# FFN layer one: an inner seven-product scheme over both token pairs for two of its seven products

## The chip, the cores and the metric

The kernel runs on one core of a Trainium2 chip. The metric is the device time of one execution in microseconds (us); less is better.

## The reference

One decoder block over 2048 tokens of width 1024, all in float32. What matters here is the feed-forward part at its end:

```
h  = x + concat[RMSNorm(PoolMix(u)), RMSNorm(StickBreakAttn(q, k, v))] @ W_out
h  = h + relu(RMSNorm(h) @ W_up) ** 2 @ W_down        # W_up 1024 x 4096, W_down 4096 x 1024
y  = RMSNorm_final(h)
```

Layer one is `relu(RMSNorm(h) @ W_up) ** 2`, layer two the product with `W_down` and the final norm.

## The kernel before

**Tokens and tiles.** The tokens are four tiles of T = 512, j = 0 to 3. Activations lie with features on the 128 partitions, so a piece is 128 x 512, 256 KB in float32. Matrices are multiplied to float32 accuracy by splitting each operand into a high and a low part (`split`, lines 140 to 144: ScalarE copies the high part, line 143; VectorE subtracts it, line 144). Each 128x128 by 128x512 block product is then three matmuls: high by high, high by low, low by high.

**Seven products.** Both feed-forward layers use a seven-product scheme of the Strassen-Winograd kind over a 2 x 2 split of tokens and of features. `PAIRS = ((0, 1), (3, 2))`: pair q = 0 is the tiles 0 and 1, pair q = 1 the tiles 3 and 2. Of the normed rows of a pair seven left operands are made (A11, A12, A22 and the sums S1 to S4), each of 512 features, that is four pieces; of the four quarters of `W_up` for a column m (0 to 15: 128 columns of its left half and the same 128 of its right half) come seven right operands. The products P1 to P7 go to three PSUM accumulators: Y takes P1, P6, P7, P4; Z takes P5, P3; X takes P2. The four results of a column are squared after relu and combined at once to the left operands of layer two, written to `sd` in DRAM.

**Layer one before, `up`.** The loop runs over `cols`, pair by pair, 16 columns each, and within a column over the seven products (`slots`, with the next column's P1 put ahead of P4). Each slot is 12 matmuls (four pieces by three) in line 1016. `load` (line 876) fetches 1 MB of `W_up` for each pair and column; `add_weights` (lines 880 to 883) makes the weight sums; `make_weights` splits them (tiles `hw`), `UA` = 4 slots ahead. `make_left` (its load is line 899) loads and splits the left operands of a pair (`sr`, `sa`). `post` reads the accumulators: copies of Y in ScalarE (line 955), sums with X and Z (lines 961, 969, 985), relu and square (lines 949, 950), outputs (line 946). During pair 0, `sums_second` norms and sums the rows of pair 1 (lines 911 to 917; tiles `hn`) and keeps them in `su`. Their norm needs the root of tiles 2 and 3: `root_last` (matmuls pm, then a chain of small operations in GpSimd, lines 208 to 218 and 815, 816) and `spread` (matmuls pr, line 225), in the slots g = 1, 6 and 10.

**Order.** Work is written in program order, but the order on each engine, and on SP's queue that issues the DMAs, comes from a scheduler which goes by its own estimate of when operands and buffers are ready; program order only sets who goes first among the ready. Pools are stacked in SBUF; a tile of a pool that is opened later waits for those tiles of closed pools whose place it takes. `begin_ffn` opens the pools of `up` while the out projection's last tile still runs (lines 172 to 174 are its matmuls, `add_acc` its sums), and `up` stops at its `yield` until `ffn` goes on with it. `down` (line 1251, its loads `wr`, `ar`) follows.

Of the kernel before, what the change touches and what calls it, by code (L numbers as in the profile page):

```python
# [8 lines left out]
F32 = mybir.dt.float32  # L9
# [16 lines left out]
G = 4  # L26
# [10 lines left out]
SR = 4  # L37
LB = 4
UA = 4
LA = 5  # L40
# [6 lines left out]
def hymba_block(ctx: ExitStack, tc: tile.TileContext, xT, gains, w_in, pool_w, w_out, w_up, w_down, out):  # L47
# [87 lines left out]
    su = [[[dram.tile([P, 2, T], F32, name=f"su{q}_{i}_{c}") for c in range(2)] for i in range(7)] for q in range(2)]  # L135
# [719 lines left out]
    def up(pools, more):  # L855

        saps, hlp, rba, rtp, srp = pools
        NM = NF // 2
        cols = [(q, m) for q in range(2) for m in range(NM)]

        what = {"P1": (A11, (0, 0), "Y", True, False), "P2": (A12, (0, 1), "X", True, True),
                "P6": (S2, (1, 1), "Y", False, False), "P5": (S1, (1, 0), "Z", True, False),
                "P7": (S3, (1, 2), "Y", False, False), "P4": (A22, (1, 3), "Y", False, True),
                "P3": (S4, (0, 2), "Z", False, True)}
        order = list(what)

        slots = [cols[0] + ("P1",)]
        for n, c in enumerate(cols):
            slots += [c + (s,) for s in ("P2", "P6", "P5", "P7")]
            slots += [c2 + ("P1",) for c2 in cols[n + 1:n + 2]]  # L870
            slots += [c + (s,) for s in ("P4", "P3")]
        raw, sums, ops, left_ops, ps, keep = {}, {}, {}, {}, {}, {}

        def load(q, m):
            raw[q, m] = (rbb if m % 2 else rba).tile([P, 4, G, P], F32, tag="rb", name="rb")
            nc.sync.dma_start(raw[q, m], w_up[m])

        def add_weights(q, m):
            b, t = raw[q, m], rtp.tile([P, 4, G, P], F32, tag="rt", name="rt")
            nc.vector.tensor_tensor(t[:, 0], b[:, 3], b[:, 0], ALU.subtract)  # L880
            nc.vector.tensor_tensor(t[:, 1], b[:, 2], t[:, 0], ALU.subtract)
            nc.vector.tensor_tensor(t[:, 2], b[:, 2], b[:, 3], ALU.subtract)
            nc.vector.tensor_tensor(t[:, 3], b[:, 1], t[:, 1], ALU.subtract)
            sums[q, m] = t

        def make_weights(g):
            q, m, s = slots[g]
            which, i = what[s][1]
            if s == "P2":
                add_weights(q, m)  # L890
            hl = hlp.tile([P, 2, G, P], F32R, tag="hw", name="hw", align_bytes=256)
            split((hl[:, 0], hl[:, 1]), (sums if which else raw)[q, m][:, i])
            ops[g] = hl

        def make_left(q, s):
            i, parts = what[s][0], []
            for c in range(2):
                r = srp.tile([P, 2, T], F32, tag="sr", name="sr")
                nc.sync.dma_start(r, su[q][i][c])
                t = saps[order.index(s)].tile([P, 2, 2, T], F32R, tag="sa", name="sa", align_bytes=256)  # L900
                split((t[:, 0], t[:, 1]), r)
                parts.append(t)
            left_ops[q, s] = parts

        SUMS, second = ("P2", "P5", "P4"), {}

        def sums_second(n, part):

            c, k = n // 2, n % 2
            new = lambda name: avp.tile([P, T], F32, tag="av", name=name)  # L910
            keep = lambda i, t: nc.sync.dma_start(su[1][i][c][:, k], t)
            add = lambda to, x, y, op: nc.vector.tensor_tensor(to, x, y, op)

            def normed_of(h, i):
                t, j = new("hn"), PAIRS[1][h]
# [513 lines left out]
```

## Time and profile before

| | |
|---|---|
| runs | 1950.17, 1945.07, 1943.7 us; median 1945.07 |
| span of the profiled execution | 1941.4 us |
| granted TensorE clock, mean | 0.998 |
| TensorE busy | 1922.7 us, 9139 matmuls |
| VectorE busy | 1267.6 us |
| ScalarE busy | 956.9 us |
| moved by DMA | 426.79 MB, mean 220 GB/s |
| matmuls of layer one (line 1016) | 2688, from 694.5 to 1309 us |

The span runs from the first to the last instruction of one profiled execution. The time of the profiled execution itself isn't listed apart from its span, so the prediction goes from the span to the median by their difference. Busy times count a matmul from its start to its modelled end, and since matmuls overlap, the distance between starts says more than the durations. The same holds for the other engines' back-to-back operations.

### The profile page before, as it was taken

The numbers are of one execution on the slowest core, as the hardware profiler recorded it, in microseconds if no ns is written. First come the engines' busy times: TensorE is split into PE (matmuls) and PEld (weight loads), VectorE is DVE, ScalarE is ACT, GpSimd is POOL, SyncE is SP. The second block draws the span as 40 slices with busy tenths as digits, with TensorE's granted clock in tenths as the row PEclk, the third lists the DMA queues.
The fourth block names the chain that finished last, engine by engine and source line by source line (L and its number), as shares of the span: only waits on it lengthen the run. The fifth ranks groups of instructions, "written<-read, shape, count | busy, mean of one in ns | idle before, by whom it ended". The sixth has DMA issues, their size and how long they took to land.

```text
span 1941.4 us, 25998 instructions
## 1 busy us (share of the span) xinstructions
PE 1922.7 (99%) x9139; PEld 1605.2 (83%) x9139; DVE 1267.6 (65%) x1882; ACT 956.9 (49%) x1544; POOL 192.0 (10%) x399
## 2 busy tenths in 40 slices
PE   9999999999999999999999999999999999999997
PEld 7888888888888888888888888878888888888887
DVE  6887799668876975777586565665454443446474
ACT  5565566455544555555575555553323233424353
POOL 0211123102111110000000000000110000213010
PEclk9999999999999999999999999999999999999999
DMA  6685686888696954677564544477885554546472
GB/s 216 206 273 180 223 279 208 266 307 285 235 378 233 338 187 155 213 243 247 181 243 159 173 141 158 145 268 288 290 284 196 192 196 151 201 153 208 148 255 89
DMA packets 164845, 426.79 MB, mean 220 GB/s; under 512 B 19680, under 2 KB 25824, under 8 KB 160608
## 3 DMA queue, kind: packets, MB, share of 16 engines
q1 hardware_dynamic: 164560, 424.77, 64.1%
q8 instruction: 74, 1.21, 0.3%
q14 instruction: 67, 0.55, 0.1%
q10 hardware_dynamic: 144, 0.26, 0.0%
HBM read 284.44 MB, written 140.51 MB: 219 GB/s over the span
## 4 chain that ended last, share of the span: by engine, by line
PE 94%; DVE 3%; DMA 2%; ACT 1%; issue 0%; SPq 0%; DVEq 0%; ACTq 0%
PE pb L1251 31%; PE pY L1016 17%; PE pd L173 8%; PE pd L172 8%; PE pd L174 8%; PE pZ L1016 8%; PE pX L1016 4%; PE po L669 2%; PE pta L658 1%; PE pm L199 1%; PE pz L611 1%; PE pz L612 1%; PE pr L225 1%; DMA wr<-in_w_down_dram 1%; PE pb L1214 1%; PE pz L640 0%
## 5 line engine op out<-in xcount | busy, mean ns | idle before, releaser
L1251 PE MATMUL pb<-ad,wd 128*128 128x512 f32 x2640 | 601.6, 390 | 1.3 <-ACT ad L143 0.7
L1251 PEld LDWEIGHTS pb<-ad,wd 128*128 128x128 f32 x2640 | 494.8, 188 | 104.6 <-ACT ad L143 1.3
L1016 PE MATMUL pY<-sa,hw 128*128 128x512 f32 x1536 | 364.3, 390 | 1.2 <-ACT u L955 1.2
L1016 PEld LDWEIGHTS pY<-sa,hw 128*128 128x128 f32 x1536 | 288.1, 188 | 61.8 <-ACT u L955 2.1
L172 PE MATMUL pd<-h,hl 128*128 128x512 f32 x752 | 299.8, 399 | 0.7 <-DVE qkr L418 0.7
L173 PE MATMUL pd<-h,hl 128*128 128x512 f32 x752 | 297.2, 395 | 0.0
L174 PE MATMUL pd<-h,hl 128*128 128x512 f32 x752 | 297.0, 395 | 0.0
L143 ACT ACTIVATE ad<-ar 128x1024 fp32r<-128x1024 f32 x112 | 117.4, 1051 | 139.4 <-PE pb L1251 116.7
L1016 PE MATMUL pZ<-sa,hw 128*128 128x512 f32 x768 | 184.6, 389 | 0.0
L144 DVE TENSOR_TENSOR ad<-ar,ad 128x1024 fp32r<-128x1024 f32 x112 | 144.3, 1293 | 55.6 <-ACT ad L143 55.6
L144 DVE TENSOR_TENSOR wd<-wr,wd 128x1024 fp32r<-128x1024 f32 x64 | 82.2, 1285 | 148.9 <-ACT wd L143 148.4
L143 ACT ACTIVATE wd<-wr 128x1024 fp32r<-128x1024 f32 x64 | 67.8, 1059 | 206.0 <-PE pb L1251 198.3
L1016 PEld LDWEIGHTS pZ<-sa,hw 128*128 128x128 f32 x768 | 144.1, 188 | 29.8
L172 PEld LDWEIGHTS pd<-h,hl 128*128 128x128 f32 x752 | 142.2, 189 | 28.3 <-DVE qkr L418 1.0
L174 PEld LDWEIGHTS pd<-h,hl 128*128 128x128 f32 x752 | 141.9, 189 | 27.9
L173 PEld LDWEIGHTS pd<-h,hl 128*128 128x128 f32 x752 | 142.0, 189 | 26.8
L143 ACT ACTIVATE hl<-raw 128x512 fp32r<-128x512 f32 x168 | 104.2, 630 | 108.2 <-PE pd L174 69.9
L144 DVE TENSOR_TENSOR hl<-raw,hl 128x512 fp32r<-128x512 f32 x168 | 114.6, 687 | 51.3 <-ACT hl L143 50.9
L144 DVE TENSOR_TENSOR hw<-rt,hw 128x512 fp32r<-128x512 f32 x128 | 87.7, 688 | 76.3 <-ACT hw L143 76.1
L1016 PE MATMUL pX<-sa,hw 128*128 128x512 f32 x384 | 93.1, 389 | 0.0
L1046 DVE TENSOR_TENSOR wr<-wr 128x1024 f32<-128x1024 f32 x32 | 39.2, 1224 | 81.0 <-DMA wr<-in_w_down_dram 78.0
L955 ACT ACTIVATE u<-pY 128x512 f32<-128x512 f32 x64 | 38.1, 595 | 103.6 <-PE pY L1016 103.3
(203 smaller groups left out, 2389.7 us busy)
## 6 DMA issues: line engine op xcount, KB each, us to landing
ar<-sd SPq DMA_DIRECT2D x112, 512.0 KB, 4.5
wr<-in_w_down_dram SPq DMA_DIRECT2D x72, 512.0 KB, 3.7
rb<-in_w_up_dram SPq DMA_DIRECT2D x32, 1024.0 KB, 6.1
sd<-a SPq DMA_DIRECT2D x128, 256.0 KB, 3.7
raw<-in_w_in_dram SPq DMA_DIRECT2D x50, 512.0 KB, 4.4
sd<-s SPq DMA_DIRECT2D x96, 256.0 KB, 3.8
raw<-in_w_out_dram SPq DMA_DIRECT2D x32, 512.0 KB, 5.6
sr<-su SPq DMA_DIRECT2D x28, 512.0 KB, 5.5
```

What stands on the lines that cost most here:

```text
L143: nc.scalar.activation(hi, src, AF.Copy)
L144: return nc.vector.tensor_tensor(lo, src, hi.bitcast(F32), ALU.subtract)
L172: nc.tensor.matmul(ps, hl[:, 0, c], hi, start=(k == 0), stop=False)
L173: nc.tensor.matmul(ps, hl[:, 0, c], lo, start=False, stop=False)
L174: mm = nc.tensor.matmul(ps, hl[:, 1, c], hi, start=False, stop=(k == n - 1))
L199: marks["pm"] = nc.tensor.matmul(pm[:, c:c + 1], ss[:, c * P:(c + 1) * P], inv[n], start=(i == 0), stop=(i == len(parts) - 1))
L225: mm = nc.tensor.matmul(pr[:, b * P:(b + 1) * P], yr[:, x, b:b + 1].to_broadcast([P, P]), identr, start=(b == 0 and x == 0), stop=(b == TB ...
L669: nc.tensor.matmul(po[:, p * 256 + to:p * 256 + to + hi - lo], vw[:, 2 * p + v], at[:, x, lo:hi], start=(p == 0 and n == 0 and x == 0), sk ...
L955: nc.scalar.activation(k[name], y, AF.Copy)
L1016: nc.tensor.matmul(t, w[:, wx, c], a[:, ax, c % 2], start=first and c == 0 and x == 0, stop=last and c == G - 1 and x == 2, skip_group_che ...
L1046: nc.vector.tensor_tensor(b, a, b, ALU.subtract)
L1251: nc.tensor.matmul(ps[q, n], t[:, wx, c, n * P:(n + 1) * P], left_[q][:, ax, c], start=(n_ in ("P1", "P5", "P2") and kk == 0 and c == 0 an ...
```

## The change

Layer one becomes three stages that go over both pairs together.

- The plain stage: P2 of both pairs, 32 products of 12 matmuls, each result copied to DRAM (`cd[q][m][0]`). Behind these products run small steps (`tasks`, `behind`): pair 1 is normed and summed and written to `su1`, and left operands are made.
- The quad stage: P5 and P3. For each of the two, the left operands of both pairs together are 1024 tokens by 512 features, and the weights of the columns k and k + 8 are taken together (a "quad"), so the product is again a 2 x 2 of blocks, and is done with seven inner products of half the depth (two pieces instead of four, so 6 matmuls each). Their operands are sums of what the plain stage wrote (`inner_left`) and sums of weight sums (`quad_sums`, then the splits `quad_early` and `quad_late`). Results go to `cd[q][m][1]` and `cd[q][m][2]`.
- The chain stage: P1, P6, P7, P4 of each column, for both pairs with one set of weights. The accumulator Y is read after each product and added to the results of the other stages that come back from `cd`; after the fourth come the sums for layer two. Two columns run interleaved.

The old body of `up` and the pools opened for it in `begin_ffn` are taken out; the diff shows what is added, without the plainest helpers.

```diff
+        def inner_left(s, i, c, sides):
+            ...
+            def load():
+                if c == 0:
+                    left_ops[s] = {n: left_tile(x) for n, x in zip(("P5", "P4", "P7", "P6", "P1", "P2", "P3"), sides)}
+                for n, q, half in (("a21", 1, 0), ("a22", 1, 1), ("a11", 0, 0), ("a12", 0, 1)):
+                    r[n] = taken(q, i, 2 * half + c, n)
+            ...
+            return (s, c), load, [first, use("P5", "s1"), use("P4", "a22"),
+                          lambda: add(r["a21"], r["a11"], r["a21"], ALU.subtract), use("P7", "a21"),
+                          lambda: add(r["s1"], r["s1"], r["a11"], ALU.subtract), use("P6", "s1"), use("P1", "a11"),
+                          use("P2", "a12"),
+                          lambda: add(r["a12"], r["a12"], r["s1"], ALU.subtract), use("P3", "a12")]
...
+        def second_sums(n):
+            ...
+            return n, load, [lambda: normed_rows(r["a21"], 1, n), lambda: normed_rows(r["a22"], 1, G + n), s1,
+                          lambda: normed_rows(r["a11"], 0, n), s3, s2, s4]
...
+        def drain():
+            while works or tasks and not tasks[0][2]:
+                behind(1, False)
...
+        def product(t, w, a, first, last):
+            n = len(w)
+            for c in range(n):
+                for x, (wx, ax) in enumerate(((0, 0), (0, 1), (1, 0))):
+                    nc.tensor.matmul(t, w[c][wx], a[c][ax], start=first and c == 0 and x == 0,
+                                     stop=last and c == n - 1 and x == 2, skip_group_check=True)
...
+        for g, (q, m) in enumerate(plain):
+            t = bank("Y", 4)
+            need((q, "P2"))
+            plain_product(t, ops.pop(g), left_ops[q, "P2"], True, True)
+            o = new("c2", copies)
+            nc.scalar.activation(o, t, AF.Copy)
+            nc.sync.dma_start(cd[q][m][0], o)
             if g == 1:
-                root_last(1, sslast, psu, "R")
-            elif g in (6, 10):
-                pr, i = psu.tile([P, T], F32, tag="R", name="pr"), g // 10
+                root_last(1, sslast, psu, "Z")
+            elif g in (2, 6):
+                pr, i = bank("Z"), g // 6
                 spread(pr, yrlast[:, i])
                 nc.scalar.activation(rlast[:, i], pr, AF.Copy)
+            if g + UA < len(plain):
+                plain_weights(g + UA)
+            if g == 4:
+                prefetch()
+            if g == 27:
+                phase[0] = 1
+            if g > 6:
+                behind(3 if g < 27 else 2)
+        del left_ops[0, "P2"], left_ops[1, "P2"]
+        drain()
+        stage.close()
+        phase[0] = 2
+        rp, up_, ep, lp = spool(stage, "rp", 2), spool(stage, "uq", 2), spool(stage, "ep", 2), spool(stage, "lp", 2)
+        av[0] = spool(stage, "avc", 15)
...
+        def quad_sums(n):
+            s, k = quads[n]
+            u = units[n] = up_.tile([P, 8, 256], F32, tag="uq", name="uq")
+            halves = u.rearrange("p (y s) n -> p y s n", y=2)
+            if s == "P5":
+                r3, r0 = (r.rearrange("p m y n -> p y m n") for r in raws_of.pop(n))
+                add(halves[:, :, 0:2], r3, r0, ALU.subtract)
+            else:
+                for x, m in enumerate((k + HM, k)):
+                    nc.sync.dma_start(halves[:, :, x], w_up[m][:, 2].rearrange("p (y c) n -> p y (c n)", y=2))
+            add(u[:, 2::4], u[:, 0::4], u[:, 1::-1], ALU.subtract)
+            add(u[:, 3], u[:, 4], u[:, 2], ALU.subtract)
+            add(u[:, 7], u[:, 5], u[:, 3], ALU.subtract)
...
+        for n in range(0, last_quad, 2):
+            if n == HM:
+                del left_ops["P5"]
+                phase[0] = 3
+            need((quads[n][0], 1))
+            for i in range(14):
+                if i < 2:
+                    quad_late(n + i)
+                    if n + 2 + i < last_quad:
+                        quad_loads(n + 2 + i)
+                if i in (2, 3) and n + i < last_quad:
+                    quad_sums(n + i)
+                if i in (6, 7) and n + i - 4 < last_quad:
+                    quad_early(n + i - 4)
+                quad_product(n + i % 2, INNER[i // 2])
+                if i % 2:
+                    behind(1)
+        del left_ops["P3"]
+        drain()
+        stage.close()
+        phase[0] = 4
+        rw, hlp = spool(stage, "rw", 2), spool(stage, "hlc", UA + 2)
+        av[0] = spool(stage, "avd", 21)
...
+        def chain_weights(g):
+            m, s = order[g]
+            b = raw[m]
+            if s == 1:
+                add(b[:, 3], b[:, 2], b[:, 3], ALU.subtract)
+                add(b[:, 2], b[:, 3], b[:, 0], ALU.add)
+                add(b[:, 1], b[:, 1], b[:, 2], ALU.subtract)
+            hl = hlp.tile([P, 2, G, P], F32R, tag="hw", name="hw", align_bytes=256)
+            split((hl[:, 0], hl[:, 1]), b[:, CHAIN[s][2]])
...
+        def post(q, m, s):
+            y = ps[q, m]
+            if s < 3:
+                t = C[q, m, (0, 2, 1)[s]]
+                add(t, y, t, ALU.add)
+                act_of(t, t)
+                put(q, m, (A11, A12, A22)[s], t)
+            else:
+                a11, a12, a22 = (C.pop((q, m, i)) for i in (0, 2, 1))
+                a21, s1, s2, s4 = (new(n) for n in ("a21", "s1", "s2", "s4"))
+                act_of(a21, y)
+                ...
...
+        for g, (m, s) in enumerate(order):
+            if s == 1:
+                for q in range(2):
+                    add(C[q, m, 2], C[q, m, 2], C[q, m, 1], ALU.add)
+            w = wts.pop(g)
+            for q in range(2):
+                if s == 0:
+                    ps[q, m] = bank("Y", 4)
+                need((q, CHAIN[s][0]))
+                plain_product(ps[q, m], w, left_ops[q, CHAIN[s][0]], s == 0, s == 3)
+                post(q, m, s)
+                behind(2)
+            if g + UA < len(order):
+                chain_weights(g + UA)
+            prepare(g + 3)
```

More of the change, by code (lines that the diff above doesn't have):

```diff
@@ L36 @@
 RATIO_TAIL = 0.6
-SR = 4
-LB = 4
 UA = 4
-LA = 5
 DA = 2
@@ L853, in sums_first @@
         later.extend(lambda c=c: sums(c) for c in range(2))
[L855 to L890, printed above, removed]
@@ L891, in make_weights @@
             hl = hlp.tile([P, 2, G, P], F32R, tag="hw", name="hw", align_bytes=256)
-            split((hl[:, 0], hl[:, 1]), (sums if which else raw)[q, m][:, i])
+            split((hl[:, 0], hl[:, 1]), r)
             ops[g] = hl
[L895 to L903, printed above, removed]
@@ L1032, in down @@
+        stage.close()
+        low.close()
     def down(pools):
```

351 lines of the change are left out of this document (232 added, 119 removed).

## The prediction

> **What bounds the kernel now.** I read the page first: span, busy shares, DMA queues.
>
> ```profile
> span 1941.4 us, 25998 instructions
> PE 1922.7 (99%) x9139; PEld 1605.2 (83%) x9139; DVE 1267.6 (65%) x1882; ACT 956.9 (49%) x1544; POOL 192.0 (10%) x399
> q1 hardware_dynamic: 164560, 424.77, 64.1%
> ```
>
> TensorE is busy 99% of the span and nothing else is over 83%. Time can be saved only by giving TensorE fewer matmuls, and only as long as it does not stand idle for it. Next the layer that is changed: TensorE's instructions of line 1016, the only matmul line in it, in the windows view, and who TensorE waited for between 694 and 1310 us in the waits view.
>
> ```profile
> 694.00:1310.00 616.00, 610.80 (x2688) 504.29 (x2688) 1.00 0.55 190
> PE pY L1016 <- ACT u L955: 1.2, 2, 0.7
> PE pb L1251 <- ACT ad L143: 0.7, 1, 0.7
> ```
>
> In 616 us TensorE waited 1.9 us for named work. So the layer as it stands has no slack to lose and no stall to remove. Last, TensorE's timeline at both ends of the layer gives the pace.
>
> ```profile
> 694.50 2.88 PE L1016 MATMUL pY<-sa,hw 128*128 128x512 f32 x12
> 697.22 2.88 PE L1016 MATMUL pX<-sa,hw 128*128 128x512 f32 x12
> ...
> 702.21 0.95 PE L199 MATMUL pm<-inv,sslast 128*128 128x1 f32 x8
> ...
> 709.05 1.00 PE L225 MATMUL pr<-identr,yrlast 128*128 128x128 f32 x8
> ...
> 726.27 1.00 PE L225 MATMUL pr<-identr,yrlast 128*128 128x128 f32 x8
> ...
> 1305.64 2.88 PE L1016 MATMUL pZ<-sa,hw 128*128 128x512 f32 x12
> 1309.22 2.21 PE L1251 MATMUL pb<-ad,wd 128*128 128x512 f32 x8 [0.70 <-ACT ad L143]
> ```
>
> A product of 12 matmuls starts 2.72 us after the one before it, so a matmul costs 0.2267 us of TensorE (the records' 0.39 us overlap). 2688 of them are 609.4 us; the layer takes 1309.22 - 694.50 = 614.7 us. The other 5.3 us are the pm and pr matmuls (3.0 us) and 2.3 us of small stalls.
>
> **Matmuls removed.** Before: 2 pairs x 16 columns x 7 products x 12 = 2688. After: the plain stage (P2) has 32 x 12 = 384, the quad stage (P5 and P3) 16 quads x 7 inner products x 6 = 672, the chain stage 16 x 4 x 2 x 12 = 1536, together 2592. Shapes stay 128x128 by 128x512, so 96 x 0.2267 = 21.8 us less TensorE work. The stages take 87.0, 152.3 and 348.2 us of it. The rest of the sum is what the new stages make TensorE wait.
>
> **VectorE's prices.** Durations overlap too; what counts is the distance of back-to-back starts.
>
> ```profile
> 1278.19 0.69 DVE L144 TENSOR_TENSOR hw<-rb,hw 128x512 fp32r<-128x512 f32 x1
> 1278.79 0.69 DVE L883 TENSOR_TENSOR rt<-rb,rt 128x512 f32<-128x512 f32 x1
> ...
> 1292.50 1.22 DVE L1046 TENSOR_TENSOR wr<-wr 128x1024 f32<-128x1024 f32 x1
> 1293.64 0.68 DVE L144 TENSOR_TENSOR hw<-rb,hw 128x512 fp32r<-128x512 f32 x1
> L917 DVE SCALAR_TENSOR_TENSOR hn<-hn,gains,rlast 128x512 f32<-128x512 f32 x16 | 11.7, 749 | 18.9 <-DMA hn<-hs 18.9
> L143 ACT ACTIVATE hw<-rt 128x512 fp32r<-128x512 f32 x128 | 80.0, 627 | 15.7 <-PE pZ L1016 12.0 <-DVE rt L881 1.9 <-PE pY L1016 1.7
> ```
>
> A 128x512 operation takes 0.60 us of VectorE, a 128x1024 one 1.14 (so by the line through both, an estimate, 0.87 for 768 and 0.33 for 256 columns); a norm I price at 0.75.
>
> **The two later stages have room.** A quad of P5 costs VectorE 1.14 + 0.60 + 2 x 0.33 for its sums, 0.87 and 1.14 for the two splits, 3 x 0.60 for adds from PSUM: 6.2 us against 9.5 us of matmuls. A column of the chain costs it 4 splits, 3 weight sums, 2 additions of the C tiles and 2 x 7 afterwards: 23 x 0.60 = 13.8 us against 21.8. A bank that ScalarE or VectorE must read before the next product goes on into it is left alone for three quad products (4.1 us) or, in the chain, 8.2 us; before, where P1's bank had one product (2.72 us), it cost the 1.2 us quoted. I put these at nothing; with the cover gone each late read would cost its lateness once per product.
>
> **The plain stage has none.** It must, beside its own weights, norm and sum the second pair and make the 14 + 14 left operands of P5 and P3. The work on tile 3 needs its root, which comes through GpSimd.
>
> ```profile
> 706.16 2.30 POOL L208 TENSOR_SCALAR v<-v 128x4 int32<-128x4 int32 x1 [29.58 <-DVE v L207]
> 713.16 0.20 POOL L816 TENSOR_TENSOR yrlast<-v,yrlast 128x4 fp32r<-128x4 f32 x1
> ```
>
> The root is done at 713.4. The diff moves its pr from after the eleventh product to after the seventh: 694.5 + 7 x 2.72 + 1.9 = 715.5, just behind, so no wait, but only 2 us of margin; the norms start at about 716.5. From there VectorE has 16 norms x 0.75 + (4 splits, 16 sums, 44 operations of the four inner lefts) x 0.60 = 50.4 us, and some 20 weight splits, 12 us: 62.4. TensorE ends the stage at 694.5 + 87.0 + 1.9 = 783.4, 66.9 us later. VectorE would have to be 93% busy. How busy it gets when it is asked for much:
>
> ```profile
> 600.00:690.00 90.00, 90.00 (x419) 75.28 (x418) 76.33 (x111) 44.22 (x69) 16.66 (x45) 1.00 0.83 293
> 786.00:946.00 160.00, 160.00 (x708) 132.51 (x707) 112.94 (x181) 87.05 (x153) 0.00 (x0) 1.00 0.69 239
> ```
>
> 0.85 in the out projection, 0.71 where the second pair is normed and summed now (there it isn't pressed). At 0.85 the 62.4 us take 73.4, to 789.9; less about 3 us of tile 2's norms and sums, which can be done ahead of 716.5: 3.5 us late.
>
> **First boundary.** Only then come the first quad's weights, and the pools overlap: the two raw tiles lie where the last tasks' rows lay, so their loads start when those end. Rows of this size land in 4.6 us:
>
> ```profile
> hn<-hs SPq DMA_DIRECT2D x16, 256.0 KB, 4.6
> rb<-in_w_up_dram SPq DMA_DIRECT2D x32, 1024.0 KB, 6.1
> ```
>
> Between 0 (freed early) and 5 us (wholly behind), I take 2. Then the sums (2.4 us) and the first split: its first matmul needs only ScalarE's part (0.63 us for 512 columns, so some 0.9 for 768), its third VectorE's, about 0.5 later: 1.4, together 3.8. So TensorE stands for 3.5 + 2 + 3.8, about 9 us; ends 0 and 18. Quad 1 is covered by quad 0's other products.
>
> **Second boundary.** The chain's raw weights are 1 MB loads of 6.1 us, behind the last quads' outputs on SP's queue unless issued early. How early such loads go when memory comes free, the chain of waits shows:
>
> ```profile
> 1283.24 6.88 DMA wr<-in_w_down_dram
> ```
>
> That load belongs to the down layer and is issued 26 us before its first product, so the order is not the program's. The first raw tile lies on space free since the middle of the quad stage. P7's left operands, however, take over tiles that P3 uses to its end, with 8 splits (4.8 us) due within 10.9 us. From 0 to 7 us; I take 1.
>
> **Third boundary.** The down layer's first rows and left operands now take over P7's tiles and the last hi/lo weights, in use until 8 us before the end and to the very end. Now TensorE waits 0.70 there, as quoted; afterwards a split of 1024 columns (ScalarE, then 1.14 on VectorE) stands in the open, beside the last column's eight sums. From 0 to 5, I take 2.
>
> Sum: -21.8 + 9 + 1 + 2 = about -10 us, with the old 2.3 us of stalls taken as staying. Against the profiled span that is 1931.4; the median of the runs shown, 1945.07, lies 3.7 above the span, so **1935**. This kernel's runs tell 0.3%, about 6 us, from no change.
>
> **Rivals.** *All is hidden* (0.12). The preparation keeps pace because every task before 716.5 runs ahead; then the three boundaries give 0 to 3 us and the time is 1923 to 1926. For it speaks the load at 1283.24, against it 93%.
>
> *VectorE becomes the bound of the plain stage* (0.15, slower). If its waits for ScalarE and for rows that go out to memory and come back hold it at the 0.71 of the second window, 62.4 us take 88, to 804.4: 21 late, and with 8.8 for load, sums and split the gap is 30. Time 1945 - 21.8 + 30 + 3 = 1956. It decides from a busy share of about 0.81: there the gap is 18.8 and with the other 3 us all is given back. What would hold it there is the DMA: the stage moves 28 raw weights, 32 outputs, 16 rows, 24 sums and 16 inner rows of 0.262 MB, 30.4 MB in 87 us or 349 GB/s. Today it moves little there; the queue row above gives 424.77 MB at 64.1% of 1941.4 us, 341 GB/s if full, and two windows that were full show:
>
> ```profile
> 580.00:590.00 10.00, 10.00 (x46) 8.29 (x45) 9.01 (x16) 4.92 (x8) 0.00 (x0) 1.00 1.03 411
> 650.00:660.00 10.00, 10.00 (x46) 8.29 (x45) 9.20 (x15) 4.12 (x7) 0.00 (x0) 1.00 0.98 357
> 694.00:786.00 92.00, 92.00 (x419) 76.59 (x419) 59.02 (x90) 51.69 (x88) 6.07 (x15) 1.00 0.43 143
> ```
>
> So the demand rises from 143 to about the limit. The Trainium skill, "DMA: Bandwidth & Descriptors", section Bandwidth, advises batches of 1 MiB or more for 75% of the peak, and this change cuts the 1 MB weight loads of this stage into 256 KB ones. The trace does not bear it out: the 411 GB/s were reached with issues of 256 and 512 KB.
>
> *The gaps cost clock as well* (0.08, no change). Where TensorE stands at the end, the granted clock falls:
>
> ```profile
> 1930.00:1935.00 5.00, 1.25 (x12) 1.08 (x10) 4.00 (x18) 2.64 (x5) 0.00 (x0) 1.00 0.53 206
> 1935.00:1941.00 6.00, 0.00 (x0) 0.00 (x0) 0.00 (x0) 0.19 (x1) 0.00 (x0) 0.52 0.51 193
> ```
>
> If after each of three gaps some 4 us run at 0.52, 2 us are lost each time: 1941. The Trainium skill, "TensorE: Matmul & The Clock Gate", Part 1, states that an idle window of about 3.4 us halves the clock and about 3.4 us of work restores it. By that rule the one gap of 9 us would add 1.7 us, an estimate, and the sum would be 1937. The trace agrees as far as the fall goes; no row shows matmuls after such a gap.
>
> *The chain runs short of tiles* (0.06, slower). It holds up to 14 C tiles and needs 8 more after a column's last product, of 21. If every column waits 1 us for an output to land, 16 us: 1951.
>
> **How the numbers follow.** The forecast has 0.59, spread over first gaps of 5 to 18 us: 1930 to 1945; of that 0.47 is under 1939, the rest within 0.3%. With *all is hidden* faster has 0.59; same is 0.12 + 0.08 = 0.20; the two slow rivals give 0.21. The range reaches from the full gain with a spread, 1922, to the first slow rival, 1956.
>
> **What would show it.** Right: 2592 matmuls in the layer at 0.2267 us; one gap of 5 to 15 us on TensorE some 89 us after its start, ended by VectorE or ScalarE on the quad weights; small gaps 150 us later and at the down layer's start; VectorE over 0.85 in the plain stage; DMA near 350 GB/s. Wrong: matmuls more than 0.2267 us apart inside the quads or the chain, stalls in the plain stage's products, a gap at the first boundary under 2 or over 20 us, or a clock under 1.00 after it.

## The result and the profile after

The changed kernel takes 1979.88 us (median; 1977.52 to 1981.89) against 1945.53 us: ratio 1.0177 [1.0161, 1.0193], slower by 34 us. The forecast of 1935 had the wrong sign, and the range ended at 1956. The page of the profile after, the lines that answer to those shown first of before:

```profile
span 1980.0 us, 26049 instructions
PE 1915.0 (97%) x9043; PEld 1588.0 (80%) x9043; DVE 1273.8 (64%) x1898; ACT 928.1 (47%) x1488; POOL 189.2 (10%) x399
q1 hardware_dynamic: 206352, 477.22, 71.0%
```

TensorE has the 96 matmuls less (9139 - 9043), is busy 7.7 us less and the span is 38.6 us longer: it stands idle or runs slow. The windows view of TensorE's instructions of line 1023, the layer's matmuls, and its timeline where each stage begins:

```profile
690.00:1340.00 650.00, 604.03 (x2592) 487.55 (x2592) 0.98 0.77 264
691.37 0.84 PE L1023 MATMUL pY<-sa,hw 128*128 128x512 f32 x3
...
802.50 1.22 PE L1023 MATMUL pY<-sa,eq 128*128 128x512 f32 x2 [9.24 <-ACT eq L142]
...
968.87 1.43 PE L1023 MATMUL pY<-sa,hw 128*128 128x512 f32 x5 [1.20 <-ACT hw L142]
...
1338.04 2.08 PE L1503 MATMUL pb<-ad,wd 128*128 128x512 f32 x4 [9.09 <-ACT ad L142]
1347.44 2.93 PE L1503 MATMUL pb<-ad,wd 128*128 128x512 f32 x6 [7.33 <-ACT ad L142]
```

2592 matmuls as counted, but the layer takes 646.7 us instead of 614.7, and the clock is 0.98 where it was 1.00. From these starts each stage's length follows (from its first matmul to the next stage's first; the last column runs to the end of the span). The forecast's column is made of its own terms: 87.0 + 1.9 + 1.0 for the second pr + the gap of 9; 152.3 + 1; 348.2 + 2 + the old 2.3; before's 1941.4 - 1309.2.

| us | forecast | after | difference |
|---|---|---|---|
| layer's first matmul at | 694.5 | 691.4 | -3.1 |
| plain stage and first boundary | 98.9 | 111.1 | +12.2 |
| quad stage and second boundary | 153.3 | 166.4 | +13.1 |
| chain and third boundary | 352.5 | 369.2 | +16.7 |
| down layer to the end | 632.2 | 642.0 | +9.8 |
| span | 1931.4 | 1980.0 | +48.6 |

No one stage has the fault. The first row's 3.1 us is not of the layer: its first matmul lies between 691.4 and 697.4 us in the profiles of this kernel and of the experiments below, none of which changes what runs before it. The next views say what each stage lost its time to.

**Plain stage.** VectorE at its end (timeline), then windows of all engines, then ScalarE and VectorE where the preparation begins:

```profile
792.24 0.69 DVE L143 TENSOR_TENSOR sa<-a,sa 128x512 fp32r<-128x512 f32 x1 [0.26 <-ACT sa L142]
799.10 1.23 DVE L870 TENSOR_TENSOR uq<-rq 128x1024 f32<-128x1024 f32 x1 [6.17 <-DMA rq<-in_w_up_dram]
...
718.00:793.00 75.00, 68.34 (x285) 53.31 (x283) 61.10 (x98) 43.62 (x79) 0.00 (x0) 0.98 0.87 313
740.00:750.00 10.00, 8.12 (x34) 5.86 (x33) 7.79 (x13) 6.41 (x13) 0.00 (x0) 0.98 1.04 393
...
715.87 0.63 ACT L142 ACTIVATE hw<-raw 128x512 fp32r<-128x512 f32 x1 [4.11 <-DMA raw<-in_w_up_dram]
717.74 0.58 ACT L1070 ACTIVATE rlast<-pZ 128x512 f32<-128x512 f32 x1
718.48 4.06 DVE L927 SCALAR_TENSOR_TENSOR hn<-hn,gains,rlast 128x512 f32<-128x512 f32 x6
722.46 0.69 DVE L143 TENSOR_TENSOR hw<-raw,hw 128x512 fp32r<-128x512 f32 x1
```

The preparation runs from 718 to 792.9, VectorE busy 61.1 us of 75, a share of 0.81. Then it stands for the first quad's raw weights. It begins at 718.5 though the root of tile 3 was there at 702.9 and its pr matmuls ended at 713.3: the copy of their result (`rlast`) is ScalarE's, which stood 4.11 us for a raw weight load ahead of it. At the start, six norms in a row hold the low part of the next plain weights back by 4 us. TensorE is busy 68.34 us of these 75, which before the change it was wholly.

**Clock.** Four windows of TensorE's matmuls, of the granted clock, with the matmul ahead of the first and of the third, and two neighbours at half clock behind the second:

```profile
748.74 4.61 PE L1023 MATMUL pY<-sa,hw 128*128 128x512 f32 x12 [1.03 <-DVE hw L143]
749.50:752.90 3.40, 3.40 (x9) 2.62 (x8) 0.50 1.03 388
797.50:807.50 10.00, 5.00 (x12) 3.98 (x13) 0.50 0.46 129
803.52 1.06 PE L1023 MATMUL pZ<-sa,eq 128*128 128x512 f32 x2
804.37 1.06 PE L1023 MATMUL pX<-sa,lq 128*128 128x512 f32 x2
827.75 1.00 PE L1023 MATMUL pY<-sa,eq 128*128 128x512 f32 x2 [1.91 <-ACT eq L142]
828.00:831.30 3.30, 3.30 (x9) 2.54 (x9) 0.51 1.01 382
1333.50:1350.00 16.50, 4.63 (x10) 3.23 (x11) 8.75 (x10) 5.06 (x5) 0.00 (x0) 0.50 1.03 381
```

(The last row lists all engines.) At half clock two matmuls take 0.85 us, 0.43 each, so each costs 0.20 us more than at full clock. 39 matmuls started in these windows (a window's count takes in one that runs over its edge): 8 us. The half clock comes in steps of 3.41 us: the four stretches here last 3.41, 10.24, 3.41 and 17.07 us.

**Quads.** TensorE's groups of instructions that use the quads' splits:

```profile
L1023 PE MATMUL pY<-sa,eq 128*128 128x512 f32 x192 | 53.5, 403 | 13.7 <-ACT eq L142 13.4
L1023 PE MATMUL pY<-sa,lq 128*128 128x512 f32 x192 | 49.3, 397 | 1.6 <-DVE z L870 1.6
```

Beside the 9.24 us at the boundary there are 4.2 us of waits for the first split (`eq`) and 1.6 for a sum (`z`). By the starts, the stalls after the boundary come to 7.3 us.

**Chain.** TensorE's instructions in the chain's later part, then rows of the waits view there (VectorE's and TensorE's, and SyncE's queue), a window of all engines, then one stall in the timeline:

```profile
1100.00:1310.00 210.00, 202.62 (x880) 164.10 (x879) 1.00 0.80 267
PE pY L1023 <- DVE c L870: 7.9, 12, 1.8
DVE c L870 <- DMA c<-cd: 50.4, 19, 5.0
DVE rw L870 <- DMA rw<-in_w_up_dram: 25.4, 10, 4.3
SPq L1220 <- ACT c L1224: 76.8, 42, 6.1
...
1100.00:1325.00 225.00, 217.06 (x943) 175.72 (x942) 137.70 (x220) 113.86 (x195) 0.00 (x0) 1.00 0.79 265
...
1155.48 0.69 DVE L870 TENSOR_TENSOR rw<-rw 128x512 f32<-128x512 f32 x1 [4.35 <-DMA rw<-in_w_up_dram]
1156.09 0.68 DVE L870 TENSOR_TENSOR c<-pY,c 128x512 f32<-128x512 f32 x1
1156.82 1.90 PE L1023 MATMUL pY<-sa,hw 128*128 128x512 f32 x7 [1.78 <-DVE c L870]
```

VectorE reads the bank only after an operation that waited for a load, here of weights (`rw`); TensorE's next product waits for the bank. TensorE's stalls that end at 1141, 1184, 1231, 1250 and 1278 us stand behind such a wait too: after it VectorE works without a pause up to the operation that TensorE waits for.

**Third boundary.** SyncE's queue in the timeline, and a row of the waits view:

```profile
1319.08 6.84 SPq L1220 DMA_DIRECT2D sd<-c  x4
1326.01 0.38 SPq L1294 DMA_DIRECT2D wr<-in_w_down_dram  x1
ACT ad L142 <- DMA sd<-s: 8.3, 1, 8.3
```

The down layer's first weight load goes out 12 us before its first product; before it went out 26 us ahead. That is the first gap. At the second, ScalarE's next split of a left operand waits 8.3 us for an output of the chain, which by the profile is still being written from the place of the split's tile.

### The profile page after: what moved, and what is told of

It reads as the page before. It is cut to its first block, busy times and chain, and to the rows that moved or that the text cites. A ratio compares the mean times of both kernels' runs of the same rounds, so it can differ in the third digit from the quotient of the medians.

```text
span 1980.0 us, 26049 instructions
## 1 busy us (share of the span) xinstructions
PE 1915.0 (97%) x9043; PEld 1588.0 (80%) x9043; DVE 1273.8 (64%) x1898; ACT 928.1 (47%) x1488; POOL 189.2 (10%) x399
## 4 chain that ended last, share of the span: by engine, by line
PE 78%; DMA 10%; DVE 7%; issue 2%; ACT 2%; SPq 1%; POOL 0%; DVEq 0%; ACTq 0%; POOLq 0%
PE pb L1503 30%; PE pY L1023 12%; PE pd L171 8%; PE pd L172 8%; PE pd L173 8%; DMA rw<-in_w_up_dram 3%; DMA c<-cd 2%; PE po L668 2%; PE pZ L1023 2%; DVE s L870 2%; PE pta L657 1%; DMA raw<-in_w_up_dram 1%; DMA rq<-in_w_up_dram 1%; DVE c L870 1%; DMA sd<-s 1%
## 5 line engine op out<-in xcount | busy, mean ns | idle before, releaser
L1503 PE MATMUL pb<-ad,wd 128*128 128x512 f32 x2640 | 603.6, 390 | 16.4 <-ACT ad L142 16.4
L1023 PE MATMUL pY<-sa,hw 128*128 128x512 f32 x1920 | 444.9, 392 | 16.3 <-DVE c L870 7.9
L1023 PEld LDWEIGHTS pY<-sa,hw 128*128 128x128 f32 x1920 | 359.3, 188 | 100.6 <-DVE c L870 13.0
L1223 ACT ACTIVATE c<-c 128x512 f32<-128x512 f32 x96 | 60.4, 629 | 145.0 <-DVE c L870 140.1
L1348 POOL TENSOR_TENSOR p<-p,res 128x512 f32<-128x512 f32 x8 | 12.1, 1528 | 738.3 <-ACT p L1354 724.0
L622 DVE TENSOR_TENSOR_SCAN pc<-sh 128x256 f32<-128x256 f32 (+1 forms) x128 | 78.1, 656 | 1.5 <-ACT sh L616 1.2
L870 DVE TENSOR_TENSOR c<-pY,c 128x512 f32<-128x512 f32 x96 | 64.7, 684 | 17.4 <-PE pY L1023 15.8
L1023 PE MATMUL pY<-sa,eq 128*128 128x512 f32 x192 | 53.5, 403 | 13.7 <-ACT eq L142 13.4
```

The lines of the kernel that those rows point to most:

```text
L622: nc.vector.tensor_tensor_scan(out_[:, ::-1], x[:, ::-1], x[:, ::-1], first, op0=ALU.mult, op1=ALU.bypass)
L1023: nc.tensor.matmul(t, w[c][wx], a[c][ax], start=first and c == 0 and x == 0, stop=last and c == n - 1 and x == 2, skip_group_check=True)
L1223: nc.scalar.activation(t, src, AF.Relu)
L1503: nc.tensor.matmul(ps[q, n], t[:, wx, c, n * P:(n + 1) * P], left_[q][:, ax, c], start=(n_ in ("P1", "P5", "P2") and kk == 0 and c == 0 an ...
```

## The experiments

All stand on the changed kernel. Medians are of four runs of each kernel, which spread by 4 to 12 us; a difference of two medians under 3 us says little. Stages are the lengths of the table above, from the profiled run.

| kernel | median us | ratio to before | plain | quads | chain | down |
|---|---|---|---|---|---|---|
| after | 1979.88 | 1.0177 [1.0161, 1.0193] | 111.1 | 166.4 | 369.2 | 642.0 |
| e1_down_places | 1971.64 | 1.0127 [1.0096, 1.0159] | 109.7 | 164.8 | 362.4 | 635.3 |
| e2_act_queue | 1984.31 | 1.0188 [1.0165, 1.0211] | 113.8 | 167.2 | 365.1 | 642.2 |
| e3_p3_late | 1974.85 | 1.0151 [1.0118, 1.0185] | 101.5 | 169.5 | 365.4 | 642.5 |
| e4_filled_gap | 1980.17 | 1.0179 [1.0154, 1.0203] | 110.4 | 163.8 | 366.5 | 642.1 |
| e6_raw_own_queue | 1976.28 | 1.0160 [1.0137, 1.0184] | 108.8 | 165.3 | 365.2 | 641.5 |
| e7_first_queue | 1968.60 | 1.0121 [1.0098, 1.0144] | 110.6 | 165.0 | 356.8 | 637.4 |
| e8_three | 1963.96 | 1.0091 [1.0075, 1.0108] | 102.2 | 168.3 | 353.4 | 637.5 |
| e9_chain_loads | 1978.76 | 1.0168 [1.0151, 1.0185] | 110.4 | 164.4 | 362.6 | 643.0 |
| e10_all | 1964.72 | 1.0107 [1.0085, 1.0129] | 110.4 | 163.8 | 356.8 | 635.6 |
| e11_three_chain | 1960.71 | 1.0078 [1.0055, 1.0100] | 101.6 | 166.0 | 358.0 | 637.1 |
| e12_three_quads | 1968.23 | 1.0116 [1.0088, 1.0144] | 100.9 | 167.2 | 369.0 | 638.1 |
| e13_three_c | 1961.61 | 1.0081 [1.0058, 1.0105] | 101.3 | 168.8 | 360.0 | 636.9 |
| e14_fewer_outputs | 1959.33 | 1.0061 [1.0038, 1.0084] | 102.4 | 164.7 | 363.7 | 636.5 |

### Third boundary: places, then the queue (e1, e7)

e1_down_places gives the down layer's pools other places, so that those needed first lie on space that is free early:

```diff
-rlp, tmp2, rs, rt, t8 = spool("rlp", 2), spool("tmp2", 2), spool("rs", 3), spool("rt", 4), spool("t8", DA + 1)
-s8, pup, rsp = spool("s8", 2 * DA + 1), spool("pup", 8), spool("rsp", 2)
+rt, rs, t8 = spool("rt", 4, side="right"), spool("rs", 3, side="right"), spool("t8", DA + 1, side="right")
+pup, s8 = spool("pup", 8), spool("s8", 2 * DA + 1)
+rlp, tmp2, rsp = spool("rlp", 2), spool("tmp2", 2), spool("rsp", 2)
```

> Theory: the two gaps of TensorE at the start of the down layer (9.1 and 7.3 us in the changed kernel) come from where its first tiles lie: on the chain's last left operands, weights and outputs. Here only the pools of the down layer are placed otherwise, its loads and weights over space that P1 and P6 have left some 11 to 22 us before the end, its left operands over the chain's raw weights. Then the first load of w_down is issued well before 1320 us in the trace, both gaps fall under 1.5 us, and the time is 1960 to 1966 (15 to 20 less than 1980, clock included). Rival: the DMA is simply full there (371 to 394 GB/s); then the loads go out earlier but land no earlier, the gaps stay over 10 us together, and the time is over 1973.

8.2 us less, between the theory's bounds and its rival's. Of the two gaps the second is gone and the first is left, and the first load is not issued earlier; TensorE's timeline and SyncE's queue in e1:

```profile
1334.29 15.92 PE L1503 MATMUL pb<-ad,wd 128*128 128x512 f32 x57 [7.79 <-ACT ad L142]
...
1316.63 6.84 SPq L1220 DMA_DIRECT2D sd<-c  x4
...
1326.25 0.38 SPq L1294 DMA_DIRECT2D wr<-in_w_down_dram  x1
```

The load stands behind outputs that wait for their data on the same queue; that its place was free is shown by the next run. e7_first_queue keeps e1 and issues the loads of the first two steps from GpSimd (here in short; `wr` and `ar` alike):

```diff
-nc.sync.dma_start(rows[q], sd[q][i][kk])
+(nc.gpsimd if not begun_[0] else nc.sync).dma_start(rows[q], sd[q][i][kk])
```

> The placing of e1_down_places, and the first two steps' loads of the down layer (wr and ar) on GpSimd's queue instead of SyncE's. Theory A: the 7.8 us gap that was left in e1 at 1334 comes from SyncE's order, in which the first wr load stood behind the last outputs; its place in SBUF is free at about 1315. Then the first wr load is issued at 1315 to 1318, the gap at the third boundary is under 2 us, and the time is 1960 to 1965 (e1: 1971.64). Theory B: the transfers of the last columns fill the DMA engines, so that an earlier issue buys nothing: the gap stays at 6 to 8 us, time 1969 to 1973.

GpSimd's and TensorE's timeline in e7:

```profile
1311.77 0.74 POOL L1294 DMA_DIRECT2D wr<-in_w_down_dram  x1 [605.81 <-DVE a L870]
...
1326.81 1.21 PE L1504 MATMUL pb<-ad,wd 128*128 128x512 f32 x4 [3.24 <-ACT ad L142]
1329.84 10.35 PE L1504 MATMUL pb<-ad,wd 128*128 128x512 f32 x34 [1.82 <-DVE ad L143]
```

The load goes out 14.5 us earlier and the gap falls from 7.8 to 5.1 us in two parts, so the order did hold the load, but two thirds of the gap had another cause: the splits of the first rows, in ScalarE and VectorE, end it now. The chain with its boundary is 5.6 us shorter than in e1: 4.6 of it are the first part of the gap (7.79 to 3.24), the rest are fewer stalls in the chain. The time, 3.0 us under e1, is between the two theories' bounds.

### First boundary: the preparation (e3, e4)

e3_p3_late makes P3's left operands in the quad stage instead of the plain one:

```diff
-            task(1, inner_left("P3", S4, c, (0, 0, 0, 0, 0, 0, 1)))
+            task(2, inner_left("P3", S4, c, (0, 0, 0, 0, 0, 0, 1)))
```

> The 28 splits and sums for P3's left operands (two tasks of 11 steps, 8 of the row loads) are made in the quad stage instead of the plain stage. Theory: they were what VectorE still had to do before the first quad's weights; without them the first boundary's gap of 9.2 us falls to 0 to 4, the plain stage's stalls shrink by a few us with the 8 loads less, and the time is 1966 to 1972. Rival: the gap hangs on the loads of the first quad's weights, which wait for tiles of the plain stage's last products; then the gap stays over 7 us and the time is 1976 to 1982. A cost can come in the quad stage, which then has 22 more steps on VectorE.

The first quad comes 101.5 us after the layer's start instead of 111.1, and TensorE's gap there falls from 9.24 us to 1.42 (a second wait, of 2.58 us, follows it):

```profile
794.28 0.74 PE L1023 MATMUL pY<-sa,eq 128*128 128x512 f32 x2 [1.42 <-ACT eq L142]
```

The quads pay 3 us of it back. So the gap did as the theory said, and the time, 1974.85, misses its 1966 to 1972 and falls just short of the rival's 1976. e4_filled_gap gives TensorE 36 matmuls more, which compute nothing that is used, behind the plain stage's last tasks:

```diff
+        t, a = bank("X"), left_ops["P5"]["P5"]
+        for i in range(36):
+            nc.tensor.matmul(t, a[:, 0, 0, 0:P], a[:, 0, 0], start=i == 0, stop=i == 35, skip_group_check=True)
```

> 36 matmuls of 128x512 whose result nobody reads fill 8.2 us of the first boundary's gap. Theory: the gap's second price is the clock, granted at half for 10 us after it; with TensorE kept busy the granted clock stays at 1.00 through 800 to 812 us, the first quads run at 0.227 us per matmul, and the time is 2 to 4 us less than the changed kernel: 1976 to 1978. Rival: the first quads wait for their weights anyway and the clock costs nothing there; then 1980, or more by what the added matmuls overhang.

```profile
803.16 1.22 PE L1023 MATMUL pY<-sa,eq 128*128 128x512 f32 x2 [5.61 <-ACT eq L142]
```

8 us more of TensorE work cost nothing: the first quad comes after 110.4 us, where it came after 111.1. With e3, where less preparation brings it forward by 9.6 us, this says that the start of the quads is set by the preparation, and that what TensorE loses or does inside the plain stage is covered by it. What the clock costs there this run doesn't tell: 5.61 us of gap were left, and the granted clock was still 0.50 from 803 to 806 us.

### The stalls inside the plain stage (e2, e6, e14)

e2_act_queue issues the outputs c2 from ScalarE:

```diff
-            nc.sync.dma_start(cd[q][m][0], o)
+            nc.scalar.dma_start(cd[q][m][0], o)
```

> The plain stage's 32 outputs are issued from ScalarE's queue instead of SP's, nothing else. Theory: the plain stage's six stalls (7.5 us above the pace, before the first boundary) arise because an output that waits for ScalarE's copy stands at the head of SP's queue (27 us of waiting there) and holds the raw weights behind it. Then ScalarE's wait for raw weights (25.5 us) falls under 8 us, the stalls under 2 us, the time to 1970 to 1974. Rival: the DMA's rate (340 to 393 GB/s from 730 to 780 us) makes the weights late; then the stalls stay and the time is 1977 to 1982, as in the changed kernel.

It fell: the stage is 113.8 us, the time 1984.31 is above the rival's bounds as well, ScalarE still waits 22.8 us for raw weights, and on SyncE's queue other waits took the place of those for c2 (18.0 us for norms, `sv<-hn`). e6_raw_own_queue moves the raw weight loads instead:

```diff
-            nc.sync.dma_start(r, w_up[plain[g][1]][:, 1])
+            (nc.gpsimd if copies else nc.sync).dma_start(r, w_up[plain[g][1]][:, 1])
```

> The plain stage's raw weight loads go on GpSimd's queue instead of SyncE's; nothing else changes. Theory A: the six stalls of the plain stage (7.5 us above the matmul pace) come from raw loads that stand behind c2 outputs in SyncE's order. Then ScalarE's waits for raw (25.5 us in 12 waits) fall below 8 us and the stalls below 2 us. The quads' start is set by the preparation in VectorE, so the first boundary's gap grows by about as much and the time falls by 0 to 4 us, to 1976 to 1980. Theory B: the transfers themselves are late, because the DMA engines are full (382 to 393 GB/s at 730 to 750 us). Then the waits for raw stay above 18 us, the stalls stay at 5 to 9 us, and the time is 1978 to 1983.

ScalarE's waits for raw weights, in the waits view of 690 to 793 us, first after, then e6:

```profile
ACT hw L142 <- DMA raw<-in_w_up_dram: 25.5, 12, 4.5
...
ACT hw L142 <- DMA raw<-in_w_up_dram: 7.3, 2, 4.0
```

The waits for the loads went, as theory A said, and the time is A's, but the stalls did not go (8 of 0.7 to 3.7 us from start to start): as an account of the stalls, neither theory. e14_fewer_outputs, on e8's base, leaves out pair 0's 16 writes of c2:

```diff
+            if q == 1:
                 nc.sync.dma_start(cd[q][m][0], o)
...
-            nc.sync.dma_start(t, cd[q][m][i])
+            nc.sync.dma_start(t, cd[q if i else 1][m][i])
```

> e8_three without the plain stage's outputs of pair 0 (16 writes of 256 KB, 4.2 MB, left out; the chain reads pair 1's in their place, so it still loads as much). Theory A: the plain stage's stalls at 724 to 750 us come from full DMA engines (share 0.99 to 1.04 there). Then ScalarE's waits for raw (24.4 us) fall below 10 us, the stalls below 3 us, and the quads start 98 to 100 us after the layer's first matmul (e8: 102.2). Theory B: ScalarE and VectorE do the weights' splits behind the preparation's, in order, and the raw loads are late because of SyncE's order: most of pair 0's outputs lie before 745 us, and the stalls stay at 6 us or more, the start at 101 to 103 us. Time by A 1958 to 1961, by B 1962 to 1966.

The stage takes 102.4 us (e8: 102.2), the stalls are as long (7.5 us by the starts in both) and ScalarE waits 27.1 us for raw weights (e8: 24.4): B in all but the time. That, 1959.33, lies in A's range, 4.6 us under e8; where this gain comes from stays open. One stall of e14, on SyncE's queue, in ScalarE and in TensorE, then one of e6, in VectorE and TensorE:

```profile
723.15 0.33 SPq L949 DMA_DIRECT2D sv<-hn  x1
...
724.04 0.40 SPq L1013 DMA_DIRECT2D raw<-in_w_up_dram  x1
...
728.76 0.63 ACT L142 ACTIVATE hw<-raw 128x512 fp32r<-128x512 f32 x1 [4.43 <-DMA raw<-in_w_up_dram]
729.45 3.15 PE L1023 MATMUL pY<-sa,hw 128*128 128x512 f32 x7 [2.47 <-ACT hw L142]
...
732.82 0.68 DVE L143 TENSOR_TENSOR hw<-raw,hw 128x512 fp32r<-128x512 f32 x1
733.55 2.89 PE L1023 MATMUL pY<-sa,hw 128*128 128x512 f32 x6 [2.00 <-DVE hw L143]
```

In e14 ScalarE's split waits for a raw load that was issued late: SyncE's queue stood until 723.15 at an output of norms, which VectorE was still making. The DMA engines were at a share of 0.54 from 720 to 730 us, so they were not full. In e6, where the raw loads have their own queue, the weights were there (ScalarE had split them at 731.7), and VectorE's part of the split stood behind norms and sums. So two causes lie one behind the other: SyncE's order with outputs in it, and the order of VectorE and ScalarE. With the first taken away the second holds TensorE no less long. Full DMA engines are not excluded for the stalls of the changed kernel at 745 to 750 us, where the share was 1.05.

### The chain (e9, e11, e13) and the quads (e12)

e9_chain_loads takes the chain's loads, of rw and of c, off SyncE's queue:

```diff
-            nc.sync.dma_start(raw[m], w_up[m])
+            nc.gpsimd.dma_start(raw[m], w_up[m])
...
-            nc.sync.dma_start(t, cd[q][m][i])
+            nc.gpsimd.dma_start(t, cd[q][m][i])
```

> In the chain stage the 1 MB weight loads rw and the loads of c come through GpSimd's queue, so that SyncE's holds only outputs there. Theory A: the nine stalls of the chain (8.9 us in all) come from loads that stand behind outputs still waiting for their data. Then SyncE's waits at these outputs stay, VectorE's waits for c (50.4 us) and for rw (25.4 us) fall below a third, the stalls fall below 3 us, and the time is 1971 to 1975. Theory B: the chain is short of tiles (avd 21): c loads wait for places, not for the queue; VectorE's waits for c stay above 30 us, the stalls at 6 us or more, time 1977 to 1983.

e11_three_chain does the same on e8's base, e13_three_c moves c alone.

> e8_three with the chain's loads on GpSimd's queue alone. Against e10 it tells what the plain stage's edit does. If the chain's stalls are gone in e8 already, the time is that of e8 within 3 us (1961 to 1967); if they are only fewer, 1957 to 1960.

> e8_three with only the loads of c in the chain on GpSimd's queue; the 1 MB loads rw stay on SyncE's. In e11, where both went there, the chain lost its stalls from 1100 us on, but had a new one of 3.15 us at 981 with 6.8 us of half clock behind it. Theory A: there c stood behind an rw load that waited for its place on GpSimd's queue. Then this start stall goes, the stalls after 1100 us stay away (under 2 us in sum), the chain with the third boundary is 353 to 355 us (e11: 358.1) and the time 1956 to 1960. Theory B: c's loads alone don't free VectorE, since rw, issued behind waiting outputs, still comes late: stalls of 3 us or more after 1100 us, time 1962 to 1966.

The windows of TensorE from 1100 to 1310 us in e9, and VectorE's waits in the chain of e13:

```profile
1100.00:1310.00 210.00, 210.00 (x928) 173.96 (x927) 1.00 0.79 278
```
```profile
DVE c L870 <- PE pY L1023: 60.3, 53, 2.5
DVE rw L870 <- DMA rw<-in_w_up_dram: 20.0, 9, 4.1
```

In all three, and in e10 below, TensorE is busy 210 of 210 us there. In the ten profiles that load c on SyncE's queue it is busy 198.1 (e12) to 209.1 us (e8; after: 202.62). Of VectorE's 50.4 us of waits for the loads of c at most 0.2 are left in the three; the waits for rw stay at 20 to 26.5 us and stall nothing from 1100 to 1310 us. So a wait for rw, which ended last at the stalls named above, stalls TensorE only where VectorE has no lead: there it waited 11.8 us for TensorE's banks, in the three 42.5 to 60.3. What took its lead were the loads of c that stood behind outputs on SyncE's queue, and with the same 21 tiles the stalls are gone. The Trainium skill, "Perfetto Trace Analysis", section DMA Optimizations, says that one engine for input DMAs and another for outputs may make sense. In the chain the trace agrees; in the plain stage (e6: 2.3 us shorter) and the quads (e12: 1.1) it gained little.

The time gained less than the stalls: e9 is 1.1 us under after by the medians, in theory B's range although the waits are A's (its profiled run, 1975.58, is the lowest of its four); e11 and e13 are 3.3 and 2.4 under e8, each between its two ranges. A new stall took part of it. In e13:

```profile
984.97 0.54 POOL L1217 DMA_DIRECT2D c<-cd  x1 [5.46 <-DVE sa L143]
...
987.61 2.90 PE L1023 MATMUL pY<-sa,hw 128*128 128x512 f32 x6 [4.41 <-DVE c L870]
```

The stall is there with rw on SyncE's queue too, so e13's theory A is wrong in that part: on GpSimd's queue c waits for its place, after VectorE's split of a left operand, not behind rw. e8's own chain (353.4 us) was almost free of stalls in the profiled run alone, which took 1956.91 us where its other three took 1963.91 to 1964.4; so the chain's stalls on SyncE's queue seem to come and go from run to run.

e12_three_quads moves the quads' weight loads, on e8's base.

```diff
-                        nc.sync.dma_start(r[:, x], w_up[m][:, part]...)
+                        nc.gpsimd.dma_start(r[:, x], w_up[m][:, part]...)
...
-                    nc.sync.dma_start(halves[:, :, x], w_up[m][:, 2]...)
+                    nc.gpsimd.dma_start(halves[:, :, x], w_up[m][:, 2]...)
```

> e8_three with the quad stage's weight loads (rq, uq) on GpSimd's queue. Theory A: the quads lose time as the chain did, with loads behind outputs in SyncE's order (there SyncE waited 29.3 us for c21 and 17.7 us for uq ahead of outputs, and VectorE 9.9 us for the loads of uq). Then VectorE's waits for uq and rq fall below 5 us in sum, the quad stage falls from 168.3 us to 163 or less, time 1957 to 1960. Theory B: the quads' short products (6 matmuls) are fed by sums and splits that VectorE and ScalarE do in order, whatever the loads: the stage stays at 166 us or more, time 1961 to 1966.

The quads take 167.2 us (e8: 168.3), VectorE's waits for rq and uq are 18.7 us together (e8: 14.8): their order on SyncE's queue is not the cause. That the splits and sums are, was only argued. The time, 1968.23, is above both ranges; the chain of the profiled run is 369.0 us (e8: 353.4), with 12.4 us of TensorE's waits for VectorE's sums in c.

### Together (e8, e10)

> e7_first_queue and e3_p3_late together. If the first and the third boundary are independent, the gains add: e3 gained 5.0 us on the changed kernel, e7 15 to 19, so 1956 to 1960. If making P3's left operands in the quad stage delays the chain, or the loads crowd one another, it is 1961 or more. Either way it stays above the kernel before (1945.5): stalls of the plain stage and the chain (7.5 and 8.9 us) are untouched.

> e8_three with both queue edits of e6_raw_own_queue and e9_chain_loads: every weight load of the plain stage and every load of the chain on GpSimd's queue. If each edit keeps the gain it had alone (plain stage 2.3 us shorter in e6, chain 6.5 us shorter in e9 by the starts), the time is 1955 to 1958. If e8's chain, which is 353.4 us from its first matmul to the down layer's (ideal 348.2), has lost its stalls already, the chain edit buys at most 2 us here and the time is 1959 to 1963. In neither case does it come under the kernel before (1946).

e8_three, e3 and e7 together, has gained 15.9 us: e3's 5.0 and e7's 11.3 add. The time is over the 1956 to 1960 expected, since e7 gained less than the 15 us put there. e10_all adds both queue edits, gains nothing further and is over both its ranges: the first quad is back at 110.4 us, where it is at 101.6 in e11, which differs in the raw loads alone. So on GpSimd's queue these cost the plain stage there the 9 us that e3 had won; why, stays open. The lowest that leaves nothing out is e11_three_chain, 1960.71, ratio 1.0078 [1.0055, 1.0100]: 19 us of the 34 are undone, and it is still slower than before. By their intervals e8 and e13 can't be told from it.

## Why the prediction was wrong

- **Matmuls removed: right.** 2592, and where nothing stalls, 0.2267 us apart: the chain's first 131.1 us hold 578 of them, 131.0 by that price. The 21.8 us are saved and spent elsewhere.
- **Plain stage: the mechanism right, the size not.** The gap of 9.24 us looks like the 9 forecast, but by luck, because two late ends cancelled: the first quad came at 802.5, not 792.4, and TensorE ended its products at 793, not 783.4. The step that failed is the preparation's end with the load behind it. The norms began 2.0 us late (718.5 for 716.5), not for the root, which came 10.5 us earlier than the 713.4 forecast, but for ScalarE's copy behind a raw load. VectorE had 61.1 us left where 59.4 stood (62.4 less the 3 done ahead; four norms and a sum, 3.6 us, did run ahead) and its share was 0.81, not 0.85: another 4.5 us. The raw loads of the first quad cost 6.2 us where 2 stood. A share of 0.81 is just the point that the rival *VectorE becomes the bound* named, where it put 18.8 us; the stage lost 21 (111.1 - 87.0 - 2.9). e3 and e4 bear this rival out.
- **Stalls inside the plain stage: at nothing in the sum.** They come from raw loads behind waiting outputs on SyncE's queue and from the weights' splits, which share VectorE's and ScalarE's order with the preparation (e6, e14). They cost no time on top as long as the preparation sets the end (e4). Where it ends sooner they count: in e3 the stage takes 101.5 us, against 89.9 without any stall.
- **"The two later stages have room": failed.** As a mean it held: VectorE was busy 137.7 of 225 us from 1100 on. But the stalls come from the order: in the chain from loads of c behind waiting outputs on SyncE's queue (e9, e11, e13), 7.9 us of waits by name and 11.7 us by the starts. In the quads there were 5.8 us of waits (13.4 for eq less the 9.24 at the boundary, and 1.6 for z) and 20 matmuls at half clock, 4.0 us. What holds eq and z late stays open: at the longest of these waits, 1.91 us, VectorE had first waited 3.82 us for raw weights and then did two splits of the chain's left operands and two other sums among the quad's own.
- **Second boundary: right**, 1.20 us for 1.
- **Third boundary: 16.4 us of gaps and 2.4 of clock, for 2.** The forecast saw the places taken over and priced only the split left in the open. It left out that the first load needs its place too, and that it queues behind outputs: the early issue at 1283.24, quoted from before, was no property of the kernel but of what was free and of what stood ahead on the queue. e1 and e7 recovered 11.3 us of it.
- ***The gaps cost clock as well*: it happened beside the others, not instead.** It had 6 us for three gaps; 39 matmuls cost 8, of which the 8 in the plain stage were covered. By the Trainium skill's rule ("TensorE: Matmul & The Clock Gate", Part 1) the first gap should add 1.7 us, an estimate; the 12 matmuls there cost 2.5. The same rule asks for an idle window of about 3.4 us: at 828.0 a wait of 1.91 us was followed by half clock, and the measurement decides.
- ***The chain runs short of tiles*: fell.** Same tiles, no stalls, once the loads had another queue.

That the rivals were given chances as if they excluded one another was a fault of its own: VectorE's bound and the clock came together, and with them a third that had no rival at all, loads behind waiting outputs.

## What to carry to other kernels

A saving in matmuls of a kernel that is 99% TensorE is worth only what the new stages' borders and orders leave: price the first load behind each border by when its place is free and by what stands ahead of it on its queue. Where preparation is to fill a stage at over 80% of an engine, reckon the next stage's start from the preparation and not from TensorE, and move out of it whatever the next stage doesn't need first: that was worth 9.6 us of start here, and 5.0 us of time. Mean shares of engines say nothing of in-order queues; look for loads behind outputs that still wait for their data.

## What the runs showed of the hardware

- A wait of TensorE of 1.91 us was followed by 3.41 us of half clock from 828.0 (8 matmuls, 0.43 us apart instead of 0.23). So were two waits of 0.85 and 1.03 us, from 749.5. In both cases about 1.9 of the 3.41 us ahead of the change were idle. A single wait of 1.78 us, at 1155, was followed by none. The clock after the gap of 9.24 us stayed at 0.50 until 807.5, 5 us into the work.
- With loads and outputs of 256 KB the DMA moved 393 GB/s at a share of 1.04, so the full rate didn't need larger transfers.
